# Short convolution by seven products, keys of the memory inside the linear attention, a DRAM tile per head

## The chip, the core and the metric

The kernel runs on one core of one Trainium2 chip. Its time is the device time of an execution in microseconds (us); three runs of the kernel before gave 1777.04 as the median, between 1776.96 and 1778.57. The engines are named as in the profile: PE multiplies matrices, DVE is the vector engine, ACT the scalar engine, POOL the general one; SP's queue issues most of the loads and stores, ACT's queue some.

## The reference

One encoder layer runs over two groups of tokens with the same weights: a sample of 512 tokens (stream S) and a prompt of 256 (stream P), together 768 columns. The model width is 1024.

```python
x = layer_norm(DN_ALPHA * x + 0.5 * swiglu(x, ffn1_w_gu, ffn1_w_down), ...)
x = layer_norm(DN_ALPHA * x + parallel_mixer(x, ...), ...)
x = layer_norm(DN_ALPHA * x + memory_cross_attention(x, mem, xa_w_q, xa_w_kv, xa_w_o), ...)
x = layer_norm(DN_ALPHA * x + 0.5 * swiglu(x, ffn2_w_gu, ffn2_w_down), ...)

def parallel_mixer(x, ...):
    h, gb, gc, q, k, v, g, lr_f, lr_b, m_conv, m_gla = jnp.split(x @ w_in, IN_OFFSETS, axis=-1)
    y_conv = (gb * short_conv(gc * h, conv_w)) @ w_conv_out
    ...
    o = o_f + o_b     # gated linear attention in both directions, 4 heads, chunks of 64 tokens
    o = o * lax.rsqrt(mean(o * o) + RMS_EPS) * gla_norm_g
    y_gla = (o * jax.nn.silu(g)) @ w_gla_out
    merged = jax.nn.sigmoid(m_conv) * y_conv + jax.nn.sigmoid(m_gla) * y_gla
    return merged @ w_out

def short_conv(u, w):
    up = jnp.pad(u, ((0, 0), (1, 1), (0, 0)))
    return up[:, :-2] * w[0] + up[:, 1:-1] * w[1] + up[:, 2:] * w[2]

def memory_cross_attention(x, mem, w_q, w_kv, w_o):
    q = (x @ w_q).reshape(B, T, XA_HEADS, XA_HEAD_DIM)      # 4 heads of 256
    k, v = jnp.split(mem @ w_kv, 2, axis=-1)                # 256 memory rows for each group
    s = einsum('bthd,bmhd->bhtm', q, k) * (XA_HEAD_DIM ** -0.5)
    o = einsum('bhtm,bmhd->bthd', softmax(s), v)
    return o.reshape(B, T, D_MODEL) @ w_o
```

`h`, `gc` and `gb` are 512 wide, so four blocks of 128 features each.

## The kernel before

**Products.** Every float32 operand is split into a rounded high part and the rest: ACT copies the high part (L84), DVE subtracts it (L85). A product is then three matmuls: high by high, high by low, low by high (`mm3`, L102). A weight of 128 x 1024 (`load_w`, L87) is loaded by SP into one of three `raw` buffers and split into one of five pairs `wh`, `wl`. `proj_T` (L107) multiplies it with the transposed tokens: 8 blocks of rows by three matmuls, 24 matmuls for a stream, results `pt`.

**Pairs of seven products.** `seven` (L409) takes two weights as a 2 x 2 block matrix against the two halves of the 768 columns (384 each) and makes the four blocks of results from seven products (the scheme of Strassen and Winograd) in place of eight: 7 x 12 = 84 matmuls of 384 columns, results `px`, `py`, `pz`. ACT takes snaps of partial results (L477), DVE adds (L484). The weights of the next pair are built meanwhile by DVE and ACT. In the mixer there are ten such pairs (L782 to L798): two of the gate `g` with Silu, eight of the gates `m_conv`, `m_gla` with Sigmoid, each stored to DRAM.

**The linear attention** (L823 to L995). For each head `gate(h)` makes the decay: a product `z` (L833), then on ACT absolute value, Exp and Ln (L834 to L837), on DVE the minimum and a subtraction (`la`, L835, L838), two scans (L840, L841), differences `dd` (L851) and `f` (L854), on ACT exponentials, on DVE `kin`, `qin`, `qst` (L862 to L866). `inner(h)` transposes `kin` (`kt`, L879), makes the inner attention `at` (L888) and the chunk states `kv` (L908), and DVE runs the recurrence `st` (L916). `outputs(h)` multiplies (`o`, L927, L931). Behind heads 1 and 3 `rms_scale` takes squares on ACT and sums on DVE (L941, L942). The steps of one head hang on one another through all engines, so PE needs other work meanwhile.

**Fillers.** A generator in the list `pending` holds such work in pieces. `fill(ns)` (L195) runs pieces until their costs, a number that each yields, exceed `ns`; `GFILL` (L30) are the three amounts in the linear attention: behind the first gate, behind each `inner`, behind each `outputs`. The filler is `conv()` (L954): for each of four blocks the products with `wm[4 + b]` (h) and `wm[8 + b]` (gc), their product, the three taps, and the product with `wm[12 + b]` (gb), multiplied into `uc`. The final order on each engine is set by a scheduler from the program's order and its dependences, not by the program's lines alone.

**The cross attention** (L1082 on). The filler here is `keys_values()` (L1110): eight pieces that each multiply one key weight with the memory (512 rows of both groups), stage the split result (`stg`) and store it to `kd` in DRAM over ACT's queue, then eight pieces for the values V, stored to `vd`. It runs between the transposes `lt` of the tokens (`to_T`, L180) and between the four rounds of sums for the query pairs, by the amounts `FILL` (L31). Four pairs of seven products make the queries; `qst` is stored to `qd` over ACT's queue. Then SP loads queries, keys and values of each head back (`fetch`, L1201; buffers of two heads at a time), PE makes scores (`sc`, L1255), transposes of the probabilities (`pT`) and outputs (`ov`). `kd`, `vd`, `qd` are one DRAM tile each for all heads (L1087 to L1089).

Of the kernel before, what the change touches and what calls it, by code (L numbers as in the profile page):

```python
# [7 lines left out]
F32 = mybir.dt.float32  # L8
# [20 lines left out]
SPREAD = {0: (0, 1), 3: (0, 1, 2, 3, 4)}  # L29
GFILL = (16000, 10000, 8000)  # L30
FILL = (14000, 14000, 6000)  # L31

# [23 lines left out]
def _encoder(ctx, tc, nc, io, out, dbg):  # L56
# [21 lines left out]
    def nid(p):  # L78
        uid[0] += 1
        return f"{p}{uid[0]}"  # L80
# [592 lines left out]


    def mixer(i):
        x1 = dp.tile([128, 6, D], F32, name="x1")
# [27 lines left out]
        def low_rank(s):  # L704
            ps = psum(nid("lr"))[:64, :s.T]
            for k in range(NK):
                nc.tensor.matmul(ps, lw[:, k, :], xh[s.name][:, k, :], start=k == 0, stop=False,
                                 skip_group_check=True)
            for k in range(NK):
                nc.tensor.matmul(ps[:32], lw[:, k, :32], xl[s.name][:, k, :], start=False, stop=k == NK - 1,  # L710
                                 skip_group_check=True)
            t = fx.tile([128, TT], F32, tag="big", bufs=3, name=nid("lrt"))[:32, :s.T]
# [54 lines left out]
        def big(nm):  # L767
            return fx.tile([128, TT], F32, tag="big", bufs=3, name=nid(nm))

        for k in range(4):  # L770
            a = []
            for q in (k, k + 4):
                x = big("x0")
                nc.vector.tensor_tensor(x[:], xh["all"][:, q, :].bitcast(F32), xl["all"][:, q, :].bitcast(F32),
                                        op=ALU.add)
                a.append(halves(x))
            last_sum = sums(X, (snap_t, sum_t), k, *a)
# [3 lines left out]

        pairs = [(w_g(2 * c), w_g(2 * c + 1), AF.Silu, silud, 2 * c) for c in range(2)]  # L782
        pairs += [(wm[16 + 2 * c], wm[17 + 2 * c], AF.Sigmoid, sigd, 2 * c) for c in range(8)]
        values(range(3), nc.vector)
        ws = weights_of(*pairs[0][:2])
        marks["dve"] = last_sum
        for n, (_, _, fn, dst, c) in enumerate(pairs):
            g1, x, u1, u2 = products(ws)
            first, second = big("first"), big("second")
            for half, (g, u) in enumerate(((g1, u1), (x, u2))):  # L790
                hc = slice(half * HT, (half + 1) * HT)
                nc.scalar.activation(first[:, hc], g, fn)
                nc.scalar.activation(second[:, hc], u, fn, scale=-1.0)
            nc.scalar.dma_start(dst[:, c, :], first[:])
            nc.scalar.dma_start(dst[:, c + 1, :], second[:])
# [20 lines left out]
        nc.sync.dma_start(glab[:], io["gla_b"])  # L816
        cw = gp.tile([128, 4, 3], F32, name="cw")
        nc.sync.dma_start(cw[:], io["conv_w"])
        attm = [gp.tile([128, TT], F32, name=f"attm{h}") for h in range(2)]
# [131 lines left out]
        co = {"S": slice(0, TS), "P": slice(TS + 1, TT + 1)}  # L951
        uo = {"S": slice(1, TS + 1), "P": slice(TS + 2, TT + 2)}

        def conv():  # L954
            for b in range(4):
                u = gp.tile([128, TT + 3], F32, tag="u", bufs=1, name=nid("u"))
                for z in (0, TS + 1, TT + 2):
                    nc.gpsimd.memset(u[:, z:z + 1], 0.0)
# [12 lines left out]
                nc.vector.scalar_tensor_tensor(c[:], u[:, 0:TT + 1], cw[:, b, 0:1], c[:], ALU.mult, ALU.add)  # L971
                nc.vector.scalar_tensor_tensor(c[:], u[:, 2:TT + 3], cw[:, b, 2:3], c[:], ALU.mult, ALU.add)
# [109 lines left out]
    def attention():  # L1082
# [14 lines left out]
        mh, ml = [mp.tile([128, NK, 512], F32R, name=f"m{p}") for p in "hl"]  # L1097
        def memory(c):

            r = wp.tile([128, 1024], F32, tag="raw", bufs=3, name=nid("raw"))  # L1100
            for n, s in enumerate(STREAMS):
                nc.sync.dma_start(r[:, n * 512:n * 512 + 512], io[f"mem{s.name}"][c])
            split(*[m[:, 2 * c:2 * c + 2, :].rearrange("p k (s t) -> p k s t", s=2) for m in (mh, ml)],
                  r[:].rearrange("p (s k t) -> p k s t", s=2, k=2))

# [3 lines left out]

        def keys_values():  # L1110
            for i in range(8):
                w = load_w(io["w_xk"][i])
                ps = proj_T(w, None, rh=[mh[:, k, :] for k in range(NK)], rl=[ml[:, k, :] for k in range(NK)], T=512)
                yield 5500
                t, h, l = staged()
                split(h, l, ps)
                nc.scalar.dma_start(kd[:, i], t[:].bitcast(F32).rearrange("p (a b) -> p a b", a=2))
            for half in range(2):
# [9 lines left out]
                for m in range(4):  # L1128
                    t, h, l = staged()
                    split(h, l, pss[m][:])  # L1130
                    t3 = t[:].bitcast(F32).rearrange("p (a h c) -> p a h c", a=2, h=2)
                    for u in range(2):
                        nc.scalar.dma_start(vd[:, 2 * half + u, m], t3[:, :, u, :])

# [10 lines left out]
        pending.append(keys_values())  # L1145
        gb = ln_params(lp, 1)
        groups = [(S, (0, 1)), (S, (2, 3)), (P, (0, 1))]
        tok_out(io["w_mix_out"], [g + (half,) for half in range(2) for g in groups], merged,
                {3 + n: [norms(s, ts, 1, gb, x2)] for n, (s, ts) in enumerate(groups)},
                [[]] * 4 + [[lambda c=c: memory(c)] for c in range(4)])  # L1150
        to_T(S, 0)
# [49 lines left out]
        def fetch(h, parts):  # L1201
            pool = ev if h % 2 == 0 else od
            for p in parts:
                if p == "q":
                    t = pool.tile([128, 2, 2, TT], F32R, tag="q", bufs=1, name=nid("q"))
                    src = qd[:, 2 * h:2 * h + 2]
                elif p == "k":
                    t = pool.tile([128, 2, 2, 512], F32R, tag="k", bufs=1, name=nid("k"))
                    src = kd[:, 2 * h:2 * h + 2]
                else:  # L1210
                    t = od.tile([128, 4, 2, 256], F32R, tag="v", bufs=2, name=nid("v"))
                    src = vd[:, h]
                last_fetch[0] = nc.sync.dma_start(t[:].bitcast(F32), src)
                tl[p, h] = t
# [3 lines left out]
        for h in range(4):  # L1218
            g1, x, u1, u2 = products(ws)
            for b, parts in ((1, (u1, u2)), (0, (g1, x))):  # L1220
                t = qs.tile([128, 2, TT], F32R, tag="qst", bufs=2, name=nid("qst"))
                for n, p in enumerate(parts):
# [4 lines left out]
                    else:  # L1227
                        ins = V.tensor_tensor(lo, p, hi.bitcast(F32), op=ALU.subtract)
                nc.scalar.dma_start(qd[:, 2 * h + b], t[:].bitcast(F32))
            marks["dve"] = ins.ins  # L1230
# [285 lines left out]
```

## Time and profile before

| | |
|---|---|
| median of three runs | 1777.04 us |
| profiled execution | 1777.92 us |
| its span in the trace | 1776.1 us |
| mean granted clock of PE | 0.994 |
| pairs of the mixer | 556.6 to 702.4 us |
| linear attention, first `z` to the last outputs | 718.6 to 859.2 us |
| transposes and keys | 994.3 to 1044.1 us |
| values V | 1044.1 to 1089.3 us |
| query pairs | 1089.3 to 1151.3 us |

The span is the time from the first to the last instruction of the profiled execution. In the views of the profile a row "a <- b" names the tile written and the tiles read; "idle before <- releaser" is how long the engine stood before the instruction and what released it. A row of the table of waits has the waiting engine and line, what it waited for, then us in total, times, and the longest. In the busy time by stretch each engine has us and number of instructions, then come the granted clock (1.00 is full), the DMA share and GB/s. A count there also takes in instructions that only reach into the stretch.

### The profile page before, as it was taken

To read this page: it belongs to the slowest core of one execution; us is meant where nothing else is said; L and a number is where in the kernel's file an instruction comes from. 1 tells how busy PE (TensorE), PEld (TensorE's weight loads), DVE (VectorE), ACT (ScalarE), POOL (GpSimd) and SP (SyncE) were. 2 spreads that over 40 slices of the span, in tenths; PEclk is the share of its full clock that TensorE was granted. 3 is DMA by queue.
4 is the path that set the end of the run, shared out by engine and by line. 5 is a ranking of instruction groups with operands and counts; after the bars stand their busy time and mean duration, and the time that the engine had idled before them with its cause. 6 is when DMAs were issued, how large, how long until landed. Compare 5 with 4: busy or idle time off the path is not lost.

```text
span 1776.1 us, 24813 instructions
## 1 busy us (share of the span) xinstructions
PE 1749.7 (99%) x9518; PEld 1607.4 (91%) x9518; DVE 1266.4 (71%) x2191; ACT 753.2 (42%) x1303; POOL 38.6 (2%) x72
## 2 busy tenths in 40 slices
PE   9999999999999999999999999979999999999998
PEld 9999999988899999888888888968899999998886
DVE  8777777597668654678785985555887777767866
ACT  6444444453245544645232343442244444444431
POOL 0000000000100000000000000020000000000002
PEclk9999999999999999999999999989999999999999
DMA  5333333687333334211464545475324333327951
GB/s 202 135 122 115 125 126 106 220 313 252 122 119 102 125 125 143 82 48 49 138 206 154 190 146 183 161 315 191 131 72 141 116 125 121 128 98 293 335 182 71
DMA packets 106038, 271.96 MB, mean 153 GB/s; under 512 B 10400, under 2 KB 32672, under 8 KB 104384
## 3 DMA queue, kind: packets, MB, share of 16 engines
q1 hardware_dynamic: 91776, 239.97, 39.1%
q10 hardware_dynamic: 14144, 30.41, 4.5%
q8 instruction: 74, 1.21, 0.3%
q14 instruction: 44, 0.36, 0.1%
HBM read 206.12 MB, written 64.23 MB: 152 GB/s over the span
## 4 chain that ended last, share of the span: by engine, by line
PE 95%; DVE 2%; DMA 2%; ACT 1%; issue 0%; SPq 0%; ACTq 0%; DVEq 0%
PE px L472 24%; PE dn L283 13%; PE py L472 12%; PE pz L472 6%; PE pt L104 5%; PE pt L103 5%; PE pt L105 5%; PE to L103 2%; PE to L105 2%; PE to L104 2%; PE dn L103 2%; PE dn L104 2%; PE dn L105 2%; PE pp L472 1%; PE lt L188 1%; PE V L105 1%
## 5 line engine op out<-in xcount | busy, mean ns | idle before, releaser
L84 ACT ACTIVATE wh<-raw 128x512 fp32r<-128x512 f32 (+2 forms) x281 | 221.0, 789 | 270.5 <-PE pt L104 83.9
L85 DVE TENSOR_TENSOR wl<-raw,wh 128x512 fp32r<-128x512 f32 (+2 forms) x281 | 248.6, 887 | 94.2 <-ACT wh L84 93.9
L283 PE MATMUL dn<-wh,ao 128*128 128x512 f32 x600 | 185.6, 390 | 0.0
L283 PEld LDWEIGHTS dn<-wh,ao 128*128 128x128 f32 x600 | 112.7, 188 | 23.4
L103 PE MATMUL pt<-xh,wh 128*128 128x512 f32 (+2 forms) x384 | 130.1, 339 | 0.0
L104 PE MATMUL pt<-xl,wh 128*128 128x512 f32 (+2 forms) x384 | 129.5, 337 | 0.0
L105 PE MATMUL pt<-xh,wl 128*128 128x512 f32 (+2 forms) x384 | 129.1, 336 | 0.0
L84 ACT ACTIVATE wh<-tt 128x512 fp32r<-128x512 f32 x156 | 93.9, 624 | 72.0 <-PE px L472 60.5
L283 PE MATMUL dn<-wl,ao 128*128 128x512 f32 x300 | 116.8, 389 | 0.0
L85 DVE TENSOR_TENSOR wl<-tt,wh 128x512 fp32r<-128x512 f32 x156 | 104.0, 685 | 3.0 <-ACT wh L84 2.2
L472 PE MATMUL px<-xh,wh 128*128 128x384 f32 x280 | 93.7, 335 | 0.0
L472 PE MATMUL px<-xh,wl 128*128 128x384 f32 x280 | 93.7, 335 | 0.0
L472 PE MATMUL px<-xl,wh 128*128 128x384 f32 x280 | 93.7, 335 | 0.0
L549 DVE SCALAR_TENSOR_TENSOR h<-sil,sum 128x384 f32<-128x384 f32 x78 | 43.5, 558 | 54.8 <-ACT sil L548 54.8
L103 PEld LDWEIGHTS pt<-xh,wh 128*128 128x128 f32 x384 | 72.8, 190 | 7.4 <-issue 0.5
L105 PEld LDWEIGHTS pt<-xh,wl 128*128 128x128 f32 x384 | 72.7, 189 | 6.4
L104 PEld LDWEIGHTS pt<-xl,wh 128*128 128x128 f32 x384 | 72.8, 190 | 6.3 <-issue 0.2
L103 PE MATMUL to<-wh,xh 128*128 128x512 f32 x192 | 75.0, 391 | 0.0
L104 PE MATMUL to<-wl,xh 128*128 128x512 f32 x192 | 74.8, 390 | 0.0
L105 PE MATMUL to<-wh,xl 128*128 128x512 f32 x192 | 74.8, 390 | 0.0
L84 ACT ACTIVATE ao<-sr 128x768 fp32r<-128x768 f32 x50 | 42.0, 844 | 68.4 <-issue 25.1
L548 ACT ACTIVATE sil<-sum 128x384 f32<-128x384 f32 x39 | 20.5, 525 | 111.4 <-DVE sum L484 111.4
(404 smaller groups left out, 4795.5 us busy)
## 6 DMA issues: line engine op xcount, KB each, us to landing
raw<-in_ffn_gu_dram SPq DMA_DIRECT2D x84, 512.0 KB, 3.5
raw<-in_ffn_dn_dram SPq DMA_DIRECT2D x64, 512.0 KB, 5.6
raw<-in_w_mix_dram SPq DMA_DIRECT2D x32, 512.0 KB, 3.5
sr<-sspill SPq DMA_DIRECT2D x32, 384.0 KB, 5.2
sspill<-hs SPq DMA_DIRECT2D x56, 192.0 KB, 1.9
hspill<-hq SPq DMA_DIRECT2D x12, 768.0 KB, 3.7
hr<-hspill SPq DMA_DIRECT2D x24, 384.0 KB, 5.9
x<-acc SPq DMA_DIRECT2D x18, 512.0 KB, 2.6
```

The costliest lines, as they stand in the source:

```text
L84: nc.scalar.activation(hi, src, AF.Copy)
L85: (lo_eng or nc.vector).tensor_tensor(lo, src, hi.bitcast(F32), op=ALU.subtract)
L103: nc.tensor.matmul(o, lh, rh, start=start, stop=False)
L104: nc.tensor.matmul(o, lh, rl, start=False, stop=False)
L105: nc.tensor.matmul(o, ll, rh, start=False, stop=stop)
L188: nc.tensor.transpose(ps[:, j * 128:(j + 1) * 128], A[:, c:c + 128], ident[:])
L283: nc.tensor.matmul(ps[t][:], l, r[:, o], start=start and k == 0 and m == 0, stop=stop and k == 1 and m == 2, skip_group_check=True)
L472: nc.tensor.matmul(ps, l[:, c], r[:, k, :], start=st and n == 0, stop=sp_ and n == 2, skip_group_check=True)
L548: nc.scalar.activation(sil[:], g, AF.Silu)
L549: ins = nc.vector.scalar_tensor_tensor(h32[:, half * HT:(half + 1) * HT], sil[:], -0.5, u, ALU.mult, ALU.mult)
```

## The change

Three things are changed, and with them the amounts of filler.

1. The products with `wm[4 + b]` and `wm[8 + b]` leave the filler. They become four pairs of seven products, put between the pairs of the Sigmoid gates (first Sigmoid, first convolution, second Sigmoid, and so on). Behind each pair DVE multiplies h and gc into `u`, ACT and DVE make the three taps, and SP stores the result to a DRAM tile `ucd`. The filler loads it from there and multiplies with `wm[12 + b]` only.
2. The keys leave the attention and become the second filler of the linear attention, behind the convolution's last products. Both memories are loaded and split there for this (into `xh`, `xl`, whose tokens are not needed by then), and again in the attention for V. The split result of a key product is held in a `raw` buffer (`kst`), and SP stores it.
3. `kd`, `vd` and `qd` become one DRAM tile per head, and the weights of the first query pair are asked for behind the last filler.

```diff
-GFILL = (16000, 10000, 8000)
-FILL = (14000, 14000, 6000)
+GFILL = (12000, 8000, 6500)
+FILL = (8000, 9000, 4500)
...
+    kd = [dp.tile([128, 2, 2, 512], F32, name=f"kd{h}") for h in range(4)]
+    def memory(c, mh, ml):
+        r = wp.tile([128, 1024], F32, tag="raw", bufs=3, name=nid("raw"))
+        for n, s in enumerate(STREAMS):
+            nc.sync.dma_start(r[:, n * 512:n * 512 + 512], io[f"mem{s.name}"][c])
+        split(...)
+    def mem_keys(mh, ml):
+        for i in range(8):
+            w = load_w(io["w_xk"][i])
+            ps = proj_T(w, None, rh=[mh[:, k, :] for k in range(NK)], rl=[ml[:, k, :] for k in range(NK)], T=512)
+            yield 5500
+            t = wp.tile([128, 1024], F32R, tag="raw", bufs=3, name=nid("kst"))
+            split(t[:, :512], t[:, 512:], ps)
+            nc.sync.dma_start(kd[i // 2][:, i % 2], t[:].bitcast(F32).rearrange("p (a b) -> p a b", a=2))
...
+        def short_conv(b):
+            def finish(g1, x, u1, u2):
+                u, c = big("u"), big("c")
+                for z in (0, TS + 1, TT + 2):
+                    nc.gpsimd.memset(u[:, z:z + 1], 0.0)
+                for o, p, m, c0, n in ((1, g1, u1, 0, HT), (1 + HT, x, u2, 0, TS - HT), (TS + 2, x, u2, TS - HT, TP)):
+                    V.scalar_tensor_tensor(u[:, o:o + n], m[:, c0:c0 + n], -1.0, p[:, c0:c0 + n], ALU.mult, ALU.mult)
+                c1 = c[:, :TT + 1]
+                nc.scalar.activation(c1, u[:, 1:TT + 2], AF.Copy, scale=cw[:, b, 1:2])
+                V.scalar_tensor_tensor(c1, u[:, 0:TT + 1], cw[:, b, 0:1], c1, ALU.mult, ALU.add)
+                V.scalar_tensor_tensor(c1, u[:, 2:TT + 3], cw[:, b, 2:3], c1, ALU.mult, ALU.add)
+                nc.sync.dma_start(ucd[:, b, :], c1)
+            return finish
...
+        con = [(wm[4 + b], wm[8 + b], short_conv(b)) for b in range(4)]
+        pairs += sig[:1] + con[:1] + sig[1:2] + con[1:2] + sig[2:3] + con[2:3] + sig[3:4] + con[3:] + sig[4:]
...
         def conv():
             for b in range(4):
-                u = gp.tile([128, TT + 3], F32, tag="u", bufs=1, name=nid("u"))
-                w = load_w(wm[4 + b])
-                for s in STREAMS:
-                    ps = proj_T(w, s)
-                    nc.scalar.activation(u[:, uo[s.name]], ps, AF.Copy)
-                    yield s.T * 10.2
-                w = load_w(wm[8 + b])
-                for s in STREAMS:
-                    ps = proj_T(w, s)
-                    nc.vector.tensor_tensor(u[:, uo[s.name]], u[:, uo[s.name]], ps, op=ALU.mult)
-                    yield s.T * 10.2
                 c = mop.tile([128, TT + 1], F32, tag="uc", bufs=4, name=nid("uc"))
-                nc.scalar.activation(c[:], u[:, 1:TT + 2], AF.Copy, scale=cw[:, b, 1:2])
-                nc.vector.scalar_tensor_tensor(c[:], u[:, 0:TT + 1], cw[:, b, 0:1], c[:], ALU.mult, ALU.add)
-                nc.vector.scalar_tensor_tensor(c[:], u[:, 2:TT + 3], cw[:, b, 2:3], c[:], ALU.mult, ALU.add)
+                nc.sync.dma_start(c[:], ucd[:, b, :])
                 w = load_w(wm[12 + b])
...
+        def keys():
+            m = [x["all"][:, :, :512] for x in (xh, xl)]
+            for c in range(4):
+                memory(c, *m)
+            yield from mem_keys(*m)
-        pending.append(conv())
+        pending.extend((conv(), keys()))
...
-        kd = dp.tile([128, 8, 2, 512], F32, name="kd")
-        vd = dp.tile([128, 4, 4, 2, 256], F32, name="vd")
-        qd = dp.tile([128, 8, 2, TT], F32, name="qd")
+        vd = [dp.tile([128, 4, 2, 256], F32, name=f"vd{h}") for h in range(4)]
+        qd = [dp.tile([128, 2, 2, TT], F32, name=f"qd{h}") for h in range(4)]
...
-        ws = weights_of(wq[0], wq[1])
         marks["dve"] = last_sum
         drain()
+        ws = weights_of(wq[0], wq[1])
```

The order of the instructions on an engine moves in three places. The first is DVE's queue behind `inner(1)`, where head 2's gate is made. `la`, `c` (the scans), `dd` and `f` are of that gate, `wl` is a weight's low half, `uc` the convolution's result, `kst` the split of a key. Before (the lines are those of the profile):

```order
878 L835 TENSOR_SCALAR la1129_7319<-z1130_7320,glab_6730 128x512
879 L835 TENSOR_SCALAR la1129_7319<-z1131_7324,glab_6730 128x256
880 L977 TENSOR_TENSOR uc1111_7210<-uc1111_7210,pt1138_7356 128x256
881 L838 TENSOR_TENSOR la1129_7319<-la1129_7319,ab1128_7318 128x768
882 L85 TENSOR_TENSOR wl1198_7807<-raw1196_7805,wh1197_7806 128x1024
883 L840 SCALAR_TENSOR_TENSOR c1132_7331<-mask0_6719,la1129_7319 64x768
884 L841 SCALAR_TENSOR_TENSOR c1132_7331<-mask0_6719,la1129_7319 64x768
885 L851 TENSOR_TENSOR dd1133_7334<-c1132_7331 64x768 x2
886 L854 TENSOR_TENSOR f1134_7335<-dd1133_7334,c1132_7331 64x11 x2
887 L85 TENSOR_TENSOR wl1204_7869<-raw1202_7867,wh1203_7868 128x1024
```

The same place of the changed kernel (its lines are some 44 higher):

```order
953 L879 TENSOR_SCALAR la1188_7774<-z1189_7775,glab_7285 128x512
954 L879 TENSOR_SCALAR la1188_7774<-z1190_7779,glab_7285 128x256
955 L882 TENSOR_TENSOR la1188_7774<-la1188_7774,ab1187_7773 128x768
956 L85 TENSOR_TENSOR kst1205_7862<-pt1204_7837,kst1205_7862 128x512
957 L884 SCALAR_TENSOR_TENSOR c1191_7786<-mask0_7274,la1188_7774 64x768
958 L885 SCALAR_TENSOR_TENSOR c1191_7786<-mask0_7274,la1188_7774 64x768
959 L895 TENSOR_TENSOR dd1192_7789<-c1191_7786 64x768 x2
960 L898 TENSOR_TENSOR f1193_7790<-dd1192_7789,c1191_7786 64x11
961 L85 TENSOR_TENSOR wl1208_7868<-raw1206_7866,wh1207_7867 128x1024
```

A weight's low half stood between `la` and the scans; now the split of key 0 stands there, and the low half of key 1's weight (`wl1208`) comes behind the scans, `dd` and half of `f`. On PE the rows that use it stand there like this (`pt1204` is key 0, `pt1209` key 1, `o1210` the outputs of head 1):

```order
4306 L103 MATMUL pt1204_7837<-xh_3422,wh1202_7832 128x512
4307 L104 MATMUL pt1204_7837<-xl_3423,wh1202_7832 128x512
4308 L105 MATMUL pt1204_7837<-xh_3422,wl1203_7833 128x512
4309 L103 MATMUL pt1209_7872<-xh_3422,wh1207_7867 128x512
4310 L104 MATMUL pt1209_7872<-xl_3423,wh1207_7867 128x512
4311 L971 MATMUL o1210_7897<-acc_3427,attm1_7288 128x128
4312 L975 MATMUL o1210_7897<-st1182_7732,qst1159_7531 64x128 x2
4313 L971 MATMUL o1210_7897<-acc_3427,attm1_7288 128x128
4314 L105 MATMUL pt1209_7872<-xh_3422,wl1208_7868 128x512
```

Two rows of key 1, which need the high half only, stand ahead of four output rows, and all other rows of key 1 and of the outputs behind the first that needs `wl1208`.

The second place is DVE's queue ahead of the first query pair. `stg1521` and `stg1522` are splits of V's second half, `wl1528` holds the first low halves of the query weights, the rows on `acc` and `qS` are sums. The changed kernel:

```order
1334 L1207 TENSOR_TENSOR acc_3427<-xh_3422,xl_3423 128x768 x2
1335 L1400 TENSOR_TENSOR acc_3427<-acc_3427 128x384
1336 L1394 TENSOR_TENSOR acc_3427<-acc_3427 128x384
1337 L85 TENSOR_TENSOR stg1521_10081<-V1505_9901,stg1521_10081 128x512
1338 L85 TENSOR_TENSOR qS1l_9876<-acc_3427,qS1h_9875 128x384
1339 L1396 SCALAR_TENSOR_TENSOR acc_3427<-acc_3427 128x384
1340 L85 TENSOR_TENSOR xl_3423<-acc_3427,xh_3422 128x384
1341 L1398 SCALAR_TENSOR_TENSOR acc_3427<-acc_3427 128x384
1342 L85 TENSOR_TENSOR stg1522_10086<-V1506_9902,stg1522_10086 128x512
1343 L85 TENSOR_TENSOR qS2l_9878<-acc_3427,qS2h_9877 128x384
1344 L85 TENSOR_TENSOR qS4l_9880<-acc_3427,qS4h_9879 128x384
1345 L85 TENSOR_TENSOR wl1528_10106<-raw1525_10101,wh1527_10105 128x512
```

Before, the splits of V's second half (`stg1503` on) stood behind the low halves of the query weights:

```order
1293 L85 TENSOR_TENSOR wl1498_10004<-raw1494_9992,wh1497_10003 128x512
1294 L85 TENSOR_TENSOR wl1500_10011<-acc_3423,wh1499_10010 128x512
1295 L85 TENSOR_TENSOR wl1500_10011<-raw1493_9991,wh1499_10010 128x512
1296 L454 TENSOR_TENSOR acc_3423<-raw1514_10156 128x512
1297 L85 TENSOR_TENSOR wl1502_10018<-acc_3423,wh1501_10017 128x512
1298 L457 TENSOR_TENSOR acc_3423<-acc_3423,raw1513_10155 128x512
1299 L85 TENSOR_TENSOR stg1503_10021<-V1477_9853,stg1503_10021 128x512
1300 L85 TENSOR_TENSOR stg1504_10026<-V1478_9854,stg1504_10026 128x512
```

So the query weights have moved from ahead of V's last splits to behind two of them.

The third place is SP's queue behind the query pairs, where queries, keys and values of the heads come back. The changed kernel, with the head in the source's name:

```order
332 L1232 DMA q1564_10408<-qd0_9104 128x3072
333 L1232 DMA q1611_10810<-qd2_9106 128x3072
334 L1232 DMA q1583_10653<-qd1_9105 128x3072
335 L1232 DMA k1584_10655<-kd1_84 128x2048
336 L1232 DMA v1585_10657<-vd0_9100 128x2048
337 L1232 DMA k1612_10812<-kd2_85 128x2048
338 L1232 DMA v1613_10814<-vd1_9101 128x2048
```

The kernel before has the same seven rows in the same order, from `qd`, `kd` and `vd`: the second of them writes the buffer that head 0's queries hold.

More of the change, by code (lines that the diff above doesn't have):

```diff
@@ L672, in ffn_fast @@
         right.close()
+    kd = [dp.tile([128, 2, 2, 512], F32, name=f"kd{h}") for h in range(4)]
[3 more added lines that the diff above has]
+            nc.sync.dma_start(r[:, n * 512:n * 512 + 512], io[f"mem{s.name}"][c])
+        split(*[m[:, 2 * c:2 * c + 2, :].rearrange("p k (s t) -> p k s t", s=2) for m in (mh, ml)],
+              r[:].rearrange("p (s k t) -> p k s t", s=2, k=2))
+    def mem_keys(mh, ml):
[6 more added lines that the diff above has]
+            nc.sync.dma_start(kd[i // 2][:, i % 2], t[:].bitcast(F32).rearrange("p (a b) -> p a b", a=2))
     def mixer(i):
@@ L767, in big @@
         def big(nm):
-            return fx.tile([128, TT], F32, tag="big", bufs=3, name=nid(nm))
+            return fx.tile([128, TT + 3], F32, tag="big", bufs=3, name=nid(nm))
         for k in range(4):
@@ L772, in mixer @@
             for q in (k, k + 4):
-                x = big("x0")
-                nc.vector.tensor_tensor(x[:], xh["all"][:, q, :].bitcast(F32), xl["all"][:, q, :].bitcast(F32),
+                x = big("x0")[:, :TT]
+                nc.vector.tensor_tensor(x, xh["all"][:, q, :].bitcast(F32), xl["all"][:, q, :].bitcast(F32),
                                         op=ALU.add)
@@ L780, in w_g, with gates, finish @@
             return io["w_g"].rearrange("a p (b c) -> p a b c", b=2)[:, :, :, c * 128:(c + 1) * 128]
-        pairs = [(w_g(2 * c), w_g(2 * c + 1), AF.Silu, silud, 2 * c) for c in range(2)]
-        pairs += [(wm[16 + 2 * c], wm[17 + 2 * c], AF.Sigmoid, sigd, 2 * c) for c in range(8)]
+        cw = g1p.tile([128, 4, 3], F32, name="cw")
+        nc.sync.dma_start(cw[:], io["conv_w"])
+        ucd = dp.tile([128, 4, TT + 1], F32, name="ucd")
+        V = nc.vector
+        def gates(fn, dst, c):
+            def finish(g1, x, u1, u2):
+                first, second = big("first"), big("second")
+                for half, (g, u) in enumerate(((g1, u1), (x, u2))):
+                    hc = slice(half * HT, (half + 1) * HT)
+                    nc.scalar.activation(first[:, hc], g, fn)
+                    nc.scalar.activation(second[:, hc], u, fn, scale=-1.0)
+                nc.scalar.dma_start(dst[:, c, :], first[:, :TT])
+                nc.scalar.dma_start(dst[:, c + 1, :], second[:, :TT])
+            return finish
+        def short_conv(b):
+            def finish(g1, x, u1, u2):
+                u, c = big("u"), big("c")
[8 more added lines that the diff above has]
+                nc.sync.dma_start(ucd[:, b, :], c1)
+            return finish
+        pairs = [(w_g(2 * c), w_g(2 * c + 1), gates(AF.Silu, silud, 2 * c)) for c in range(2)]
+        sig = [(wm[16 + 2 * c], wm[17 + 2 * c], gates(AF.Sigmoid, sigd, 2 * c)) for c in range(8)]
+        con = [(wm[4 + b], wm[8 + b], short_conv(b)) for b in range(4)]
+        pairs += sig[:1] + con[:1] + sig[1:2] + con[1:2] + sig[2:3] + con[2:3] + sig[3:4] + con[3:] + sig[4:]
         values(range(3), nc.vector)
@@ L786, in mixer @@
         marks["dve"] = last_sum
[L787 to L795, printed above, removed]
+        for n, (_, _, finish) in enumerate(pairs):
+            finish(*products(ws))
             if n + 1 < len(pairs):
@@ L1097, in attention @@
         mh, ml = [mp.tile([128, NK, 512], F32R, name=f"m{p}") for p in "hl"]
[L1098 to L1104, printed above, removed]
         def staged():
@@ L1108, in staged, with mem_values @@
             return t, t[:, :512], t[:, 512:]
[L1110 to L1117, printed above, removed]
+        def mem_values():
             for half in range(2):
@@ L1132, in keys_values @@
                     for u in range(2):
-                        nc.scalar.dma_start(vd[:, 2 * half + u, m], t3[:, :, u, :])
+                        nc.scalar.dma_start(vd[2 * half + u][:, m], t3[:, :, u, :])
         def norms(s, ts, i, gb, dst):
@@ L1143, in ln_params @@
             return load_ln(lambda nm: pool.tile([128, 512], F32, tag="gb", bufs=4, name=nm), i)
-        pending.append(keys_values())
+        pending.append(mem_values())
         gb = ln_params(lp, 1)
@@ L1149, in attention @@
                 {3 + n: [norms(s, ts, 1, gb, x2)] for n, (s, ts) in enumerate(groups)},
-                [[]] * 4 + [[lambda c=c: memory(c)] for c in range(4)])
+                [[]] * 4 + [[lambda c=c: memory(c, mh, ml)] for c in range(4)])
         to_T(S, 0)
```

15 lines of the change are left out of this document (5 added, 10 removed).

## The prediction

> **What bounds the kernel now.** The head of the page comes first, then the table of waits of the tensor engine, PE.
>
> ```profile
> span 1776.1 us, 24813 instructions
> PE 1749.7 (99%) x9518; PEld 1607.4 (91%) x9518; DVE 1266.4 (71%) x2191; ACT 753.2 (42%) x1303; POOL 38.6 (2%) x72
> PE 95%; DVE 2%; DMA 2%; ACT 1%; issue 0%; SPq 0%; ACTq 0%; DVEq 0%
> PE sc L103 <- DMA k<-kd: 12.6, 1, 12.6
> PE py L472 <- ACT acc L477: 1.8, 1, 1.8
> PE o L931 <- DVE st L916: 1.1, 1, 1.1
> ```
>
> PE is busy 99% of the span, and the chain that ended last is 95% PE. So a saved matmul is saved time, but only 26 us of idle are there to win, half of it in one wait (the scores wait for head 1's keys), and every new wait of PE lengthens the run. The next view is the busy time by stretch: the ten pairs of seven products; four spans of the linear attention between one head's `kt` and the next (the first begins at `z`); one filler piece of 256 columns; one of 512.
>
> ```profile
> core 0: us, PE busy (x) PEld busy (x) DVE busy (x) ACT busy (x) POOL busy (x), PEclk, DMA share, GB/s
> 556.60:702.40 145.80, 145.80 (x842) 145.76 (x841) 85.16 (x136) 74.25 (x141) 0.00 (x0) 1.00 0.36 127
> 718.60:741.50 22.90, 22.90 (x126) 19.90 (x125) 16.49 (x19) 13.96 (x18) 0.00 (x0) 1.00 0.21 71
> 741.50:776.30 34.80, 34.80 (x238) 29.76 (x237) 26.27 (x42) 17.85 (x28) 1.15 (x10) 1.00 0.18 58
> 776.30:811.20 34.90, 34.90 (x239) 29.85 (x238) 30.09 (x56) 19.30 (x30) 0.80 (x4) 1.00 0.10 32
> 781.24:784.11 2.87, 2.87 (x26) 2.87 (x25) 1.38 (x4) 2.80 (x7) 0.00 (x0) 1.00 0.03 6
> 784.11:789.58 5.47, 5.47 (x27) 4.51 (x25) 5.07 (x14) 4.52 (x6) 0.00 (x0) 1.00 0.00 0
> ```
>
> PE never waits in these, since the convolution's products fill the gate chains. The cover is thin on the other side: in 776.30:811.20 DVE is busy 30.1 of 34.9 us.
>
> **The products that move.** Removed are eight weights of one 512-column and one 256-column piece: 8 x (5.47 + 2.87) = 66.7 us. Added are four pairs of 84 matmuls at 145.80/842 = 0.173 us: 58.2 us. That saves **8.5 us** if the pairs stay without gaps. I take no gap: in the pair stretch DVE is busy 8.5 and ACT 7.4 of 14.56 us a pair. A convolution pair adds to DVE three products of 769 columns in all and two sums, and to ACT one scaling:
>
> ```profile
> 774.14 1.02 DVE L972 SCALAR_TENSOR_TENSOR uc<-u,cw,uc 128x769 f32<-128x769 f32 x1
> ```
>
> That is about 3.3 us of DVE, inside the 6 us free. The 44.6 us of key products (8 x 24 x 0.23) only change place.
>
> **What the keys do as filler.** These rows are DVE after head 1's `kt` at 776.2, which I call T, and ACT beside them.
>
> ```profile
> 782.61 6.03 DVE L916 SCALAR_TENSOR_TENSOR st<-st,f,kv 64x128 f32<-64x128 f32 x16 [2.44 <-ACT st L914]
> 788.67 1.14 DVE L835 TENSOR_SCALAR la<-z,glab 128x512 f32<-128x512 f32 x2
> 790.06 0.95 DVE L838 TENSOR_TENSOR la<-la,ab 128x768 f32<-128x768 f32 x1
> 790.93 1.22 DVE L85 TENSOR_TENSOR wl<-raw,wh 128x1024 fp32r<-128x1024 f32 x1
> 792.06 1.74 DVE L840 TENSOR_TENSOR_SCAN c<-mask,la 64x768 f32<-64x768 f32 x1
> 793.84 1.75 DVE L841 TENSOR_TENSOR_SCAN c<-mask,la 64x768 f32<-64x768 f32 x1
> 795.62 1.94 DVE L851 TENSOR_TENSOR dd<-c 64x768 f32<-64x768 f32 x2
> 801.99 0.95 DVE L942 TENSOR_REDUCE ms<-sq 128x6 f32<-128x768 f32 x1
> 786.89 0.85 ACT L837 ACTIVATE ab<-ab 128x768 f32<-128x768 f32 x1
> 792.53 1.06 ACT L84 ACTIVATE wh<-raw 128x1024 fp32r<-128x1024 f32 x1 [2.15 <-PE pt L104]
> 800.73 1.59 ACT L941 ACTIVATE sq<-acc 128x768 f32<-128x768 f32 x2
> ```
>
> Before, a weight's low half (`wl`) was split a product or two ahead, one of them at T+14.7, ahead of the scans. In the new order DVE reaches `wl` of key 1 only behind the low half of key 0's result (`kst`, about 0.7), both scans, `dd` and `f`. From T: `st` ends at 12.5, `la` at 14.6, `kst` 15.2, scans 18.7, `dd` 20.7, `f` 20.9, `wl` **22**. PE has meanwhile done `kt`, `at`, `kv` and `z` (5.1 by the same trace) and key 0 (5.6): it is through at 10.7. Its next rows, two of key 1, need `wh`, which stands on ACT behind Ln (T+11.6) and the copy of key 0's result (0.6): 13.2. Wait 2.5. Four short output rows follow, and the third key row needs `wl`: wait about 7.6. Key 2's `wh` stands behind two copies of the outputs and the two squares (1.59), its `wl` behind the reduces (0.95 each): 3.1 behind the outputs' end. Key 3's halves can be made only after key 2's result has been copied and split, 0.6 + 1.06 + 1.2 less two rows: 2.5. Head 1 stalls 15.7 us in all. Head 2 has the same rows without the reduces: 2.3, 6.7, 2.2 and 2.5, so 13.7. Ahead of head 0 only three pieces (5.5 + 2.9 + 5.5) stand against a gate chain that these durations make some 15.4 (4.6 on ACT up to Ln, 1.0 for `la`, 3.5 for the scans, 1.9 and 0.4 for `dd` and `f`, 1.8 for an exponential and `kin`, and the hand-overs): 1.5. Head 3 keeps a wait like today's 1.1. Sum 32.4, less 1.1: **+31 us**.
>
> Bounds: below, DVE's own stall alone in heads 1 and 2 (7.6 + 6.7, with what ACT adds hidden): 14. Above, the same chains with each semaphore hand-over as long as the 0.1 to 0.3 us between rows of different engines here: 36. I take 31, since each row has its duration in this trace and an engine runs its queue in the printed order.
>
> **The clock after a stall.** The granted clock is 1.00 except behind two waits: the 1.8 us one at 1095.8 and the 12.6 us one.
>
> ```profile
> 1097.60:1101.30 3.70, 3.70 (x12) 3.70 (x13) 0.96 (x2) 1.97 (x4) 0.00 (x0) 0.55 0.41 142
> 1168.35:1173.12 4.77, 4.77 (x23) 4.77 (x23) 0.86 (x2) 0.85 (x4) 0.00 (x0) 0.51 1.01 426
> 854.00:858.00 4.00, 2.90 (x24) 1.74 (x25) 3.75 (x12) 1.03 (x2) 0.00 (x0) 1.00 0.00 0
> ```
>
> Twelve matmuls took 3.70 us in place of 12 x 0.173 = 2.08: 1.6 us lost behind a wait of 1.8; the 1.1 us wait in the last row cost nothing. The change makes some eight waits over 1.8 us in the linear attention and the attention's start. A slow matmul only costs where PE is what ends last, which is so behind each key, and a wait of 2.2 to 2.5 need not fall so that it counts. I take five times 1.6: **+8 us**, between 0 and 16.
>
> [...]
>
> **The start of the attention.** Eight filler pieces of V are left of sixteen. DVE's last sums and the first query weights come closer together, and the new order puts `wl` of the first pair behind the last sums and two splits of V's second half. Before, it stood at 1069.34, twenty us ahead of the pair.
>
> ```profile
> 1057.92 1.82 DVE L1188 TENSOR_TENSOR acc<-xh,xl 128x768 f32<-128x768 f32 x2
> 1069.34 0.68 DVE L85 TENSOR_TENSOR wl<-raw,wh 128x512 fp32r<-128x512 f32 x1
> 1096.55 0.60 ACT L84 ACTIVATE stg<-V 128x512 fp32r<-128x512 f32 x1 [3.90 <-DMA vd<-stg]
> 1097.05 0.49 ACT L477 ACTIVATE acc<-py 128x384 f32<-128x384 f32 x1
> ```
>
> The last two rows are the present fault: ACT stood 3.9 us on a store of V, and the pair's snap behind it was late. With the stage's rows put into the new order, DVE is through with the transposes at about 1027.7 of the present clock and has four rounds of sums before it (the row of 1.82 and eight of 0.47 each, 5.5 us), then a split of V and `wl`: 1051.5. PE is through with V at 1047: wait 4.4. The next weights stand behind the other two splits, whose buffers wait for stores: 2.7. And V's second half waits for its banks: 2.8. Together 9.9 in place of the 1.8 and its slow clock (1.6): **+6 us**, from 0 (all of it under the eight pieces) to +13 (a store as slow as the one above once more).
>
> **The wait for head 1's keys.** Separate DRAM tiles would let head 1's queries and keys load early. But the sync engine's queue is as before: head 2's query load, which waits for the scores of head 0 to free its buffer, stands ahead of head 1's.
>
> ```profile
> 1155.80 0.80 SPq L1213 DMA_DIRECT2D q<-qd  x2
> 1156.65 0.43 SPq L1213 DMA_DIRECT2D k<-kd  x1
> ```
>
> All are issued once the scores of head 0 end (1155.7). The two query tiles of 128 x 3072 and the keys of 128 x 2048 floats are 4.2 MB, so at the 426 GB/s of the clock row at 1168.35 alone 9.8 of the 12.6 us. I count **0**; without this wait and its slow clock (4.77 in place of 22 x 0.12 = 2.64) it would be -14.7.
>
> **Sum.** The profiled execution took 1777.9 us (span 1776.1 and 1.8 around it), 0.9 over the median. 1777.9 - 8.5 + 31 + 8 + 6 = 1814; from the median, **1813 us**.
>
> **Rivals.** (1) The splits come in time: ACT and DVE have idle time in sum (DVE 30.1 of 34.9), and if only DVE's bound of 14 us in the linear attention, half of the start's and half the clock's remained, the time is 1777 - 8.5 + 14 + 3 + 4 = 1790. Against it is the order, in which the scans stand ahead of the split. (2) Faster: keys are hidden altogether. If the loads and splits of key weights are done while PE runs the convolution's own products, PE waits as little as today, and 8.5 us stay won: 1768; it decides from a wait of under 8.5 us in all. For it: each key gives 5.6 us of cover and a split costs only 1.2. Against: a key's `wl` is asked for 11 us before DVE gets to it. (3) The head 1 loads do come early, since the program names them first: 1813 - 14.7 = 1798. Against: the printed queue. (4) The start is worse, with slow V stores and half clock after each wait: +13 and +16 in place of +6 and +8 give 1828.
>
> **How the numbers follow.** Forecast 0.55 (1800 to 1826); rival 1 0.20, of which 0.03 ends within 0.2% of today; rival 2 0.12, of which 0.02 within 0.2%; rival 3 0.07; rival 4 0.06. The range 1786 to 1828 holds forecast, rivals 3 and 4 and most of 1. About 0.2%, 3.6 us, is what a measurement of this kernel can tell from no change. Faster 0.10, same 0.05, slower 0.85.
>
> **What would show it.** In the profile after: fourteen pairs of 14.56 us with no wait in `px`, `py`, `pz`; in the linear attention two waits of PE near 7 us on `wl`, others of 2 to 3 us on `wh`, some 32 us in all, and the granted clock at 0.5 behind the long ones; `sc` still waiting 12 us for `k`; and waits at the first query pair. I am wrong if DVE splits key 1's `wl` before the scans, if the wait for `k` is gone, or if the pairs show gaps.

## The result, and the profile after

The changed kernel took 1820.76 us, median of four runs (1819.94 to 1821.72), against 1777.0 of the kernel before on the same chip: a ratio of 1.0249, 95% interval 1.0236 to 1.0262. The forecast was 1813, the range 1786 to 1828. The head of the page and the first rows of the table of PE's waits:

```profile
span 1819.2 us, 24830 instructions
PE 1758.6 (97%) x9470; PEld 1616.0 (89%) x9470; DVE 1294.6 (71%) x2247; ACT 767.5 (42%) x1331; POOL 38.6 (2%) x72
PE 91%; DVE 5%; ACT 2%; DMA 1%; issue 1%; ACTq 0%; POOL 0%; DVEq 0%; SPq 0%; POOLq 0%
PE pt L105 <- DVE wl L85: 13.6, 6, 6.1
PE sc L103 <- DMA k<-kd: 12.9, 1, 12.9
PE pt L103 <- ACT wh L84: 11.5, 6, 2.5
PE px L472 <- DVE wl L85: 5.0, 1, 5.0
PE pz L472 <- ACT wh L84: 1.8, 1, 1.8
```

The span is 43.1 us longer. PE's idle (span less busy) grew from 26.4 to 60.6 us, and 25 us of it is key products that wait for their own weight: the first and the third wait. The wait of the scores for head 1's keys is there as before (12.9 us, 12.6 before). PE's busy time grew too, by 8.9 us, although its work became less: that is the clock, and something in the pairs. The stretches show where, in PE's busy time, granted clock, DMA share and GB/s: the fourteen pairs; the linear attention from `z` to the first `kt`, then heads 0 to 3, each from its `kt` on; V; the query pairs.

```profile
core 0: us, PE busy (x), PEclk, DMA share, GB/s
557.04:763.25 206.21, 206.21 (x1177) 1.00 0.35 121
779.61:795.42 15.81, 14.32 (x76) 1.00 0.08 30
795.42:824.92 29.50, 29.50 (x212) 1.00 0.07 21
824.92:879.40 54.48, 40.22 (x190) 0.81 0.21 77
879.40:928.70 49.30, 37.33 (x190) 0.86 0.24 86
928.70:942.13 13.43, 12.07 (x106) 1.00 0.45 160
1076.10:1124.64 48.54, 48.54 (x227) 1.00 0.42 136
1124.64:1194.57 69.93, 62.52 (x338) 0.95 0.49 174
```

Head 1 lasts 54.5 us, of which PE is idle 14.3, head 2 49.3 with 12.0. DVE there, and one row of ACT:

```profile
832.68 6.03 DVE L960 SCALAR_TENSOR_TENSOR st<-st,f,kv 64x128 f32<-64x128 f32 x16 [0.51 <-ACT st L958]
840.87 0.68 DVE L85 TENSOR_TENSOR kst<-pt,kst 128x512 fp32r<-128x512 f32 x1
841.47 1.74 DVE L884 TENSOR_TENSOR_SCAN c<-mask,la 64x768 f32<-64x768 f32 x1
845.02 1.94 DVE L895 TENSOR_TENSOR dd<-c 64x768 f32<-64x768 f32 x2
847.09 1.21 DVE L85 TENSOR_TENSOR wl<-raw,wh 128x1024 fp32r<-128x1024 f32 x1
838.19 1.05 ACT L84 ACTIVATE wh<-raw 128x1024 fp32r<-128x1024 f32 x1
```

With T = 824.9, `wl` of key 1 begins at T+22.2, and PE, which has waited for it since 842.2, goes on at T+23.4, when it is done; the forecast had it done at T+22. This is the order that stands ahead of the prediction, run as printed.

### The profile page after: what moved, and what is told of

Its sections match the earlier page's. It is cut to its first block, busy times and chain, and to the rows that moved or that the text cites. A ratio compares the mean times of both kernels' runs of the same rounds, so it can differ in the third digit from the quotient of the medians.

```text
span 1819.2 us, 24830 instructions
## 1 busy us (share of the span) xinstructions
PE 1758.6 (97%) x9470; PEld 1616.0 (89%) x9470; DVE 1294.6 (71%) x2247; ACT 767.5 (42%) x1331; POOL 38.6 (2%) x72
## 4 chain that ended last, share of the span: by engine, by line
PE 91%; DVE 5%; ACT 2%; DMA 1%; issue 1%; ACTq 0%; POOL 0%; DVEq 0%; SPq 0%; POOLq 0%
PE px L472 26%; PE py L472 13%; PE dn L283 13%; PE pz L472 7%; PE pt L105 3%; PE pt L103 3%; PE pt L104 3%; PE pp L472 3%; PE to L103 2%; PE to L105 2%; PE to L104 2%; PE dn L104 2%; PE dn L105 2%; PE dn L103 2%; DVE st L960 1%; PE lt L188 1%
## 5 line engine op out<-in xcount | busy, mean ns | idle before, releaser
L105 PE MATMUL pt<-xh,wl 128*128 128x512 f32 (+2 forms) x320 | 115.3, 360 | 13.6 <-DVE wl L85 13.6
L103 PE MATMUL pt<-xh,wh 128*128 128x512 f32 (+2 forms) x320 | 116.0, 362 | 11.7 <-ACT wh L84 11.5
L104 PE MATMUL pt<-xl,wh 128*128 128x512 f32 (+2 forms) x320 | 114.4, 358 | 0.0
L472 PE MATMUL px<-xh,wl 128*128 128x384 f32 x312 | 105.0, 336 | 5.0 <-DVE wl L85 5.0
L472 PE MATMUL px<-xh,wh 128*128 128x384 f32 x312 | 104.8, 336 | 0.0
L472 PE MATMUL px<-xl,wh 128*128 128x384 f32 x312 | 104.7, 335 | 0.0
L105 PEld LDWEIGHTS pt<-xh,wl 128*128 128x128 f32 x320 | 62.5, 195 | 23.2 <-DVE wl L85 16.0
L103 PEld LDWEIGHTS pt<-xh,wh 128*128 128x128 f32 x320 | 62.6, 196 | 21.2 <-ACT wh L84 13.7
L104 PEld LDWEIGHTS pt<-xl,wh 128*128 128x128 f32 x320 | 62.9, 196 | 6.8
L548 ACT ACTIVATE sil<-sum 128x384 f32<-128x384 f32 x39 | 20.5, 525 | 111.4 <-DVE sum L484 111.4
```

Of the source, the lines that this page charges most:

```text
L103: nc.tensor.matmul(o, lh, rh, start=start, stop=False)
L104: nc.tensor.matmul(o, lh, rl, start=False, stop=False)
L105: nc.tensor.matmul(o, ll, rh, start=False, stop=stop)
L472: nc.tensor.matmul(ps, l[:, c], r[:, k, :], start=st and n == 0, stop=sp_ and n == 2, skip_group_check=True)
L548: nc.scalar.activation(sil[:], g, AF.Silu)
```

## The experiments

Runs of the kernel before beside them had medians of 1776.6 to 1777.6 us. All ratios are against it.

**The weight asked for one key earlier.** The generator loads and splits the next key's weight ahead of this key's products.

```diff
+        nw = load_w(io["w_xk"][0])
         for i in range(8):
-            w = load_w(io["w_xk"][i])
+            w = nw
+            nw = load_w(io["w_xk"][i + 1]) if i < 7 else None
             ps = proj_T(w, None, ...)
```

> The changed kernel, with the weight of the next key loaded and split ahead of the products of this key. Theory A (the stalls come from where the splits of a key's weight stand: behind the result of the key before and the next head's gate): the two waits on wl of 6.1 and 5.4 us go, the waits on wh ahead of them (2.0 and 2.5) and behind them (1.5 to 2.3) mostly too; idle of PE in the linear attention falls from 29 us to under 12 and the time lost at half clock there from 10.6 to under 4: about 1797 us. Theory B (DVE and ACT have too much to do in this stage, wherever the splits stand): the waits only move, idle stays over 22 us: 1814 to 1821 us.

Measured: 1788.15 us, ratio 1.0065 (1.005 to 1.008), 9 us better than theory A had it; idle of PE in the linear attention 4.9 us in place of 29.1, and the loss at half clock there about 4 in place of 10.6. (This loss is an estimate: the time from start to start of the matmuls issued at half clock, less that of their forms at full clock.) So the engines had time enough; theory B falls. But this edit also shifts which buffer of the ring each load takes, so it does not tell the program's order from the ring.

**A buffer of its own for the staged key.** The program's order stays; only `kst` leaves the ring of three `raw` buffers.

```diff
-    def mem_keys(mh, ml):
+    def mem_keys(mh, ml, pool):
...
-            t = wp.tile([128, 1024], F32R, tag="raw", bufs=3, name=nid("kst"))
+            t = pool.tile([128, 1024], F32R, tag="kst", bufs=1, name=nid("kst"))
...
-            yield from mem_keys(*m)
+            yield from mem_keys(*m, gp)
```

> The changed kernel, with the staged result of a key in a buffer of its own in the linear attention's pool in place of one of the three raw buffers; the program's order is that of the changed kernel. Theory R (the late splits come from the ring: the result of a key takes the buffer that the weight after next is loaded into, so that its load waits for a store): the splits move ahead of the gate, idle of PE in the linear attention falls from 29 us to under 8, time at half clock likewise: 1786 to 1791 us, as with the weight asked for one key ahead. Theory E (the place of load_w behind the result of the key before, in the program, is the cause): idle stays near 29 us, 1815 to 1821 us.

Measured: 1787.49 us, 1.0054 (1.0037 to 1.0071). DVE at the same place of this run, and PE from `z` to the last outputs:

```profile
832.23 1.22 DVE L85 TENSOR_TENSOR wl<-raw,wh 128x1024 fp32r<-128x1024 f32 x1
834.12 6.03 DVE L960 SCALAR_TENSOR_TENSOR st<-st,f,kv 64x128 f32<-64x128 f32 x16 [0.33 <-ACT st L958]
841.24 1.22 DVE L85 TENSOR_TENSOR wl<-raw,wh 128x1024 fp32r<-128x1024 f32 x1
```

```profile
779.90:909.40 129.50, 123.15 (x768) 0.97 0.30 106
```

`wl` of key 1 is split ahead of the recurrence `st`, the next one ahead of the scans. Idle is 6.4 us. The ring is the cause. In SP's queue the loads of the key weights stand like this, first in the changed kernel, then in this run:

```profile
827.84 0.33 SPq L93 DMA_DIRECT2D raw<-in_w_xk_dram  x1
841.58 0.33 SPq L692 DMA_DIRECT2D kd<-kst  x1
844.19 0.33 SPq L93 DMA_DIRECT2D raw<-in_w_xk_dram  x1
```

```profile
823.48 1.47 SPq L93 DMA_DIRECT2D raw<-in_w_xk_dram  x2
828.09 0.33 SPq L93 DMA_DIRECT2D raw<-in_w_xk_dram  x1
```

In the changed kernel the staged key 0 takes a buffer of the ring, so key 1's weight gets the buffer behind it, which the last piece of the memory holds until its split ends at 827.82: it is asked for at 827.84, in this run at 824.6 (the second of the two loads in the row). Key 2's weight waits for the store of key 0 and is asked for at 844.19, here at 828.09. For key 1 a load that comes 3.2 us later goes with a split that stands 15 us later in DVE's queue (847.09 against 832.23), behind the gate. That the scheduler puts it there because it orders an engine by what is ready is my reading; no run shows its reckoning.

**The address of the pairs' operands.** In the changed kernel the products P5, P6, P3 and P7 take 176.7 ns a matmul from start to start, in all fourteen pairs, P1, P2 and P4 173.4 to 173.9; before, all took 173.3. Their token operands lie behind three tiles `big`, which grew from 768 to 771 floats.

```diff
-            return fx.tile([128, TT + 3], F32, tag="big", bufs=3, name=nid(nm))
+            return fx.tile([128, TT + 16], F32, tag="big", bufs=3, name=nid(nm))
```

> The changed kernel, with the tile 'big' of 784 floats in place of 771, so that the tiles placed behind it start at a multiple of 64 bytes again. Theory of the address: the products P5, P6, P3 and P7, whose token operand lies behind these tiles, go from 176.7 ns a matmul back to 173.3: 14 pairs x 48 x 3.4 ns = 2.3 us less, 1818.5 us. Rival (the longer pair stage's loads and stores slow the matmuls): still 176.7 ns, 1820.8 us.

Measured: 173.3 ns again, and the pairs shorter by 2.35 us, as expected:

```profile
core 0: us, PE busy (x), PEclk, DMA share, GB/s
557.15:761.01 203.86, 203.86 (x1177) 1.00 0.35 123
```

But the whole took 1821.17 us, not 1818.5. The 2.35 us were given back in the linear attention: a wait of 1.5 us for the first `kt` is in both traces, yet behind it the padded kernel ran at half clock, the unpadded one at full. The first row is the padded kernel, behind its wait, the second the changed one:

```profile
795.00:801.60 6.60, 6.60 (x46) 0.50 0.02 4
```

```profile
797.20:803.80 6.60, 6.60 (x71) 1.00 0.01 4
```

46 against 71 matmuls in 6.6 us. So the size of the tiles ahead of the operands sets the 3.4 ns, and the rival falls; that it is the multiple of 64 bytes that counts is not tested apart. The gain in the whole went into that half clock; why it stood behind the wait in one kernel and not in the other, no run shows.

**The queue's order.** One block is added around the loads of the head after next.

```diff
             if h < 2:
-                fetch(h + 2, "qk")
+                with tc.issue_after(last_fetch[0].ins):
+                    fetch(h + 2, "qk")
```

> The changed kernel, with head 2's query and key loads put behind head 1's loads and head 0's values in SP's queue. Theory of the queue (head 1's loads wait only because head 2's stand ahead of them): head 1's query and keys, 2.6 MB, are issued at the end of the query pairs, some 4.5 us earlier and with nothing ahead, so the wait of sc for k falls from 12.9 to about 4 us and the half clock behind it shrinks: about 1811 us. Rival (the tiles of head 1 only come free then, or the transfers need that long in any order): the wait stays over 10 us, 1818 to 1821 us.

> The kernel before, one DRAM tile for all heads, with head 2's loads behind head 1's and head 0's values in SP's queue and nothing else changed. Theory (only the queue's order holds head 1's loads back; a load waits only for the stores of its own part of a DRAM tile): the wait of 12.6 us and the 2.1 us at half clock behind it go: about 1763 us. Rival (with one tile a load of head 1 waits for the stores of the last pair too): a wait of 4 us and over stays, 1768 to 1772 us.

Measured: on the changed kernel 1808.39 us, 12.4 less; on the kernel before 1763.28, ratio 0.992 (0.9905 to 0.9935), 13.7 less. In SP's queue of the first of them:

```profile
1187.54 0.33 SPq L1232 DMA_DIRECT2D q<-qd  x1
1189.62 0.32 SPq L1232 DMA_DIRECT2D k<-kd  x1
1202.26 0.32 SPq L1232 DMA_DIRECT2D q<-qd  x1
```

Head 1's loads are issued 8 to 10 us ahead of the end of the query pairs (1197.8), earlier than I had expected, and head 2's behind the scores of head 0. No wait of `sc` for `k` is left in either. The kernel before has one DRAM tile for all heads and wins as much, and separate tiles alone left the wait at 12.9 us: they are not what holds or frees these loads.

**The keys back in the attention.** First with `kst` still in the ring, then staged as before the change (`stg`, ACT's queue) with the two repairs above.

```diff
-        pending.extend((conv(), keys()))
+        pending.append(conv())
...
-        pending.append(mem_values())
+        pending.extend((mem_keys(mh, ml), mem_values()))
```

In the second run the last line is this, and the store of a key goes over ACT's queue:

```diff
+        pending.extend((mem_keys(mh, ml, lambda: staged()[0]), mem_values()))
...
-            nc.sync.dma_start(kd[i // 2][:, i % 2], t[:].bitcast(F32).rearrange("p (a b) -> p a b", a=2))
+            nc.scalar.dma_start(kd[i // 2][:, i % 2], t[:].bitcast(F32).rearrange("p (a b) -> p a b", a=2))
```

> The changed kernel with the keys back in the attention and the old amounts of filler; the seven-product pairs of the convolution and the DRAM tiles stay. Theory A: no waits on wl or wh of keys, but the gate chain has only the four products of the convolution's third weight as cover: 15.4 us to the first kt, some 23 for each head and 13 at the end make 98 us against 70 us of PE work, so 28 us of idle, in waits of kt for kin and o for st, and some 8 us at half clock; the attention's start as before. About 1805 us. Rival (the key splits are the whole trouble and the stage has cover enough without keys): idle under 5 us, about 1772 us.

> The convolution's pairs alone, with the padded tile and the queue's order mended: all keys are back in the attention, staged and stored over ACT's queue as in the kernel before, and the amounts of filler are the old ones. Theory (without keys the linear attention has too little work beside the gates): 25 us of idle and 11 us at half clock there, as in the run with the keys back; none of the attention's 27 us of that run, whose weights waited for the staged results in the raw ring: 1763 - 8.5 + 25 + 11 = 1790 us. If the attention shows its 27 us all the same, the ring was not their cause: over 1815.

Measured: 1855.16 us, ratio 1.0443 (1.0427 to 1.0458), and 1796.14, 1.0104 (1.0089 to 1.0119). The first was 50 us worse than expected: the linear attention had 26 us of idle, near the 28 that I had worked out, but lost some 16 at half clock in place of 8, and the attention had 27 more of idle, which I had not seen coming, on `wh` and `wl` of the keys and `wh` of V's first weight, and 13 us lost at half clock behind them. In the second these 27 are gone. It changes both the staging buffer and the queue of the store; the runs with four to seven keys below keep SP's queue for the store, stage the attention's keys in `stg`, and have no wait of a key on its weight there either. So these waits came from the ring as well. The second run's linear attention from `z` to the outputs, and the waits there:

```profile
777.20:894.90 117.70, 90.67 (x576) 0.78 0.08 27
```

```profile
PE kt L923 <- DVE kin L906: 16.2, 3, 7.7
PE o L975 <- DVE st L960: 10.5, 3, 5.0
```

27 us of 118 idle, and some 15 us lost at half clock; 25 and 11 were expected, and these two differences make up the 6 us over 1790. Without the convolution's products and without keys the gates have too little cover. The convolution's pairs save work only if something else fills this stage.

**How many keys.** With the three repairs (own `kst`, padded tile, queue), the rest of the keys staged in the attention in `stg`. With fewer than eight keys the third amount of `FILL` is 6000 in place of 4500 too; no run parts this from the number of keys.

```diff
-            yield from mem_keys(*m)
+            yield from mem_keys(*m, range(n), ...)
...
-        pending.append(mem_values())
+        pending.extend((mem_keys(mh, ml, range(n, 8), ...), mem_values()))
```

> The three repairs together: a buffer of its own for a key's staged result, the tile 'big' padded to 784 floats, head 2's loads behind head 1's. If they are independent: 1788 less 12.4 for the queue and 2.3 for the address: about 1773 us; 1770 to 1776, as the half clock falls with the phase of its window. The attention's start keeps its 6.8 us of waits. If the time won in one place comes back in another: over 1780 us.

> As the run with the three repairs, but only four keys in the linear attention, the other four in the attention ahead of V, staged as before. Theory (the start of the attention waits because too little PE work is left there beside the sums): the waits of px on wl (5.0) and pz on wh (1.8) and their half clock go, and the linear attention, whose gate chain lasts some 23 us a head, still has cover for most: about 1766 us. Rival (the linear attention needs all eight keys as cover): 10 us or more of new waits there, 1774 us and over.

> The run with the three repairs, but six keys in the linear attention and two in the attention ahead of V. With eight keys the linear attention had 4.9 us of idle and the attention's start 6.6; with four it was 16.6 and 2.5. If the gate chains of heads 1 and 2 need some 10 us of cover more than four keys give, six are enough: idle of the linear attention under 7 us, and 11 us more work at the start are enough for the sums: about 1764 us. If each key that is taken out opens a wait of its own length: 1770 us and over.

> As the run with six keys, with five in the linear attention and three in the attention. Head 1 then has four and head 2 one: 5 to 6 us of new waits in head 2, and none at the attention's start: about 1768 us. If five give cover enough: 1762.

> As the run with six keys, with seven in the linear attention and one in the attention. The wait of kt for kin in head 2 (2.6 us with six, none with eight) and the half clock around it (10 us, about 4 us lost) go; at the attention's start one key of 5.6 us stands against the 6.6 us of waits that eight keys left: 1 to 2 us stay. About 1760 us. If the start's waits come back with their half clock as with eight keys: 1769 us.

| keys in the linear attention | median us | ratio, interval |
|---|---|---|
| 8 | 1772.07 | 0.9969 (0.9956 to 0.9982) |
| 7 | 1765.49 | 0.993 (0.9916 to 0.9944) |
| 6 | 1764.72 | 0.9926 (0.9912 to 0.9941) |
| 5 | 1776.04 | 0.9995 (0.9985 to 1.0004) |
| 4 | 1781.07 | 1.0017 (1.0007 to 1.0026) |

Eight came out as the sum of the repairs, and six at its 1764. The phase that the range for eight (1770 to 1776) names as its reason is not shown by any run; shown is that the same wait of 1.5 us had a clock of 0.50 behind it in the padded kernel and 1.00 in the changed one. Four missed its 1766: `kt` and `o` wait 6.2 and 5.7 us for the gates, as the rival said. Five was expected at 1768: `kt` waits 7.2 us, the clock is at half for 20.5 us in all, and the query pairs wait 2.7 us where no wait was expected. Seven was expected at 1760: `kv` waits 2.6 us for ACT, 10.2 us at half clock stay, and the query pairs wait some 2.5 us in place of 1 to 2. With six, the linear attention, the start of the attention and the query pairs:

```profile
777.00:900.60 123.60, 115.89 (x728) 0.94 0.27 94
1031.90:1093.30 61.40, 61.40 (x289) 1.00 0.45 160
1093.30:1151.60 58.30, 58.30 (x338) 1.00 0.69 249
```

The start and the pairs have no idle left; the linear attention keeps 7.7 us and a clock of 0.94. That beats both kernels, but not the kernel before with its queue mended (1763.28; the intervals of the ratios overlap): what the pairs save, some 8.5 us, goes into that idle and clock.

## Why the prediction was right, by its steps

Direction and cause held; the time came 8 us over the forecast. The span's 43.1 us, by the distance between the first matmuls of the stages:

| stretch | change, us |
|---|---|
| pairs of the mixer and values | +60.6 |
| linear attention | +22.1 |
| from there to the output product, which lost some rows to it | -2.8 |
| transposes, keys and V | -44.8 |
| query pairs | +8.0 |
| scores and the rest | 0.0 |

**Work**, forecast -8.5: the four pairs cost 60.6 in place of 58.2, as fourteen pairs have four slower products each (2.35 us). With 66.7 us of removed products -6.1. Nobody waits in the pairs: that step was right.

**Waits in the linear attention**, forecast 32.4 (its four parts add up to 32.0): 29.1. By place: 1.5 against 1.5 at the first `kt`, none ahead of head 1, 14.3 against 15.7 in head 1, 12.0 against 13.7 in head 2, 1.4 against 1.1. The two long waits on `wl` were 6.1 and 5.4 us, forecast 7.6 and 6.7, and the waits on `wh` ahead of them 2.0 and 2.5, forecast 2.5 and 2.3. So the order gave the size of the waits; why the order is so, the ring, the prediction did not name. Its rival that the splits come in time (1790) is what the kernel becomes once the staged key leaves the ring (1787.49). Its rival of keys hidden altogether (1768) did not come even then: 6.4 us of idle and the waits at the attention's start stay.

**The clock**, forecast +8: by the estimate above the matmuls issued at half clock took 10.6 us longer in the linear attention than their forms at full clock, and 3.0 in the query pairs against 1.6 before; in the scores 1.3 against 2.1. Together +11, mis-sized by 3. As in the prediction's row, where it was a wait of 1.8 us, short waits were enough here: behind five of 1.5 to 2.5 us in the linear attention the clock was 0.50, though not each time (behind one of 1.6 us, from 920.7 on, it was 1.00). The prediction let a wait of 2.2 to 2.5 us go without cost; here the clock was 0.50 behind both of that length (2.33 and 2.48 us).

**The start of the attention**, forecast +6 (9.9 us of waits in place of 1.8 and its slow clock of 1.6): idle 7.4 against 1.8, so +5.6. The first wait was 5.0 (4.4 forecast), the second 1.8 (2.7), but V's second half waited for no bank (2.8): the stretch of V is 48.54 us, all busy. And the slow clock, which the term takes off, did not go; it is the 3.0 above. That the term came out near is luck: two errors cancel.

**The wait for head 1's keys**, forecast 0: 12.9 against 12.6. The rival that the program's order would win falls, and the queue's experiment shows why.

The terms add up to -6.1 + 28.0 + 11 + 5.6 + 0.3 = 39 of 43. Most of the other 4 is in the linear attention, whose busy time at full clock is 2.6 us more than its products before would make. It stands in the rows ahead of the waits: a matmul of 512 columns that another follows takes 227 ns from start to start, one ahead of a wait is counted as busy to its end, 388 ns. Sixteen rows of the linear attention are followed by a wait, and this comes to 2.7 us for them, so a wait costs some 0.16 us more than its idle. The rest, under 2 us, stays open.

## What to carry to other kernels

A staging buffer put into a ring that also feeds loads pushes the loads behind it to later buffers. Here a load that came 3.2 us later went with a split 15 us later: look where each split stands in the engine's order, not only how busy the engine is. Look also at what stands ahead of a transfer in its queue: here a DRAM tile of its own left the wait for head 1's keys at 12.9 us, and a new order of the loads took it away. Work taken off PE, the bound engine here, was won only where the stage that it covered had other cover: without the keys there the linear attention had 27 us of idle.

## What was not expected of the hardware

A matmul's token operand behind tiles of 771 floats was 3.4 ns slower (176.7 against 173.3, alternating between 174 and 179), and back at 173.3 with 784.

Waits of one length did not always have the same clock behind them. In the changed kernel's trace waits of PE of 1.98, 2.33, 1.63, 2.48 and 1.45 us end at 839.3, 861.7, 871.4, 892.6 and 912.5, and the granted clock was 0.50 from 839.4 to 853.0, 863.3 to 866.7, 873.5 to 876.9, 894.0 to 904.2 and 914.5 to 917.9; the two long waits on `wl` (6.1 and 5.4 us) fall into the first and the fourth of these stretches. Behind another wait of 1.63 us, which ends at 922.3, and one of 1.49 us, which ends at 795.4, it stayed 1.00. The wait of 1.5 us for the first `kt` had at least 6.6 us at 0.50 behind it in the padded kernel and none in the changed one, which reached it 2.2 us later. What parts these cases is not shown by any run.
